# Weight sums formed again instead of reloaded, and seven chunks' state contributions formed earlier

## The chip, the cores and the metric

The kernel runs on one core of a Trainium2 chip. The metric is the device time of one execution in microseconds (us). TensorE (PE) multiplies matrices, VectorE (DVE) and ScalarE (ACT) work on tiles, GpSimd (POOL) too, and SyncE (SP) and ACT issue most transfers between the device memory and the core's own.

## The reference

One block of a network on 2048 tokens of width 1024, with 256 tokens of context ahead of it, all in 32 bits:

```python
hx = modulate(rmsnorm(x, norm1[l]), sh1, sc1)
px, qx, kx, vx, ox, gx = project(hx, w_in[l], conv_qk[l], gate_bias[l])
hc_m, st_f, st_b = mlstm_bidir(qc, kc, vc, gc, zero_state(bsz), zero_state(bsz))
hx_m, _, _ = mlstm_bidir(qx, kx, vx, gx, st_f, st_b)
pool_x = pool_mixer(px.reshape(bsz, rows, GRID_W, POOL_WIDTH), pool_w[l], pool_scale[l])
mix_x = jnp.concatenate([pool_x, mlstm_output(hx_m, ox, head_norm[l])], axis=-1) @ w_out[l]
x = x + g1 * mix_x
x = x + g2 * swiglu(modulate(rmsnorm(x, norm2[l]), sh2, sc2), w_up[l], w_down[l])
...
c_new = decay[..., None, None] * c0 + jnp.einsum('bhs,bhsv,bhsd->bhvd', wk, vc, kc)
n_new = decay[..., None] * n0 + jnp.einsum('bhs,bhsd->bhd', wk, kc)
```

The projection `w_in` has parts for the pool mixer, for queries and keys (through a convolution over three tokens), values, an output gate o, and the gates of the recurrence. The recurrence runs over the tokens forwards and backwards, in chunks; the last two lines are its state. What a chunk adds to the state (the einsum of its keys, values and weights `wk`) depends on that chunk alone; the states then follow from one another by a decay.

## The kernel before, in words

**Chunks.** The kernel takes chunks of 128 tokens: 16 of x, two of the context. For each it needs the keys transposed and weighted for both directions (`delta_a`), the products with the values of four heads (`delta_b`), copies by ACT into the state slots `ST`, and, once the neighbours are there, the decay step (`scan_step`, DVE). Slot `ST(k)` holds the forward state ahead of chunk k in partitions 0 to 63 and the backward state ahead of chunk 15 - k in the other 64.

**Units.** The pool, convolution (queries and keys) and o parts of `w_in` are computed in units of 256 columns, first for one half of the activations and then for the other. A unit multiplies two by two blocks with seven products in place of eight, and so needs seven weight operands: three are blocks of the weights, four (`SUMS`: 4, 3, 5, 2) are sums of them. Each operand is split into a high part (a cast by ACT, `wh`) and a residual (a subtraction on DVE, `wl`), and each of the seven products is 12 matmuls of 128x512 (lines 642 to 644). `operands` makes them: `wsum` forms a sum on DVE. In the first half the operands of the four sums are also stored (`keep_=s_w[w]`, line 631); in the second they are loaded again (`kept`, line 597) and only half of the second raw block is loaded. The order is: first half convolution, o, pool; second half pool, convolution, o. The activation tiles `h0` to `h6` are loaded once for a half.

**The second half's o units.** The two last units run side by side, product by product. Between the products and in their middle a hook calls `chunk_step`, which loads a later chunk's keys and values (`load_ahead`), forms `delta_a` of one chunk and `delta_b` of the one before. The state slots lie in tiles that reuse `h0`, `h1` and `h5`, so they can be written once the products with those are done. The chunks come in the order

```python
seq = [(True, cc) for cc in range(NCC)] + [(False, cc) for i in range(NCH // 2) for cc in (i, NCH - 1 - i)]
```

that is, two of the context, then 0, 15, 1, 14 and so on. What is not done by the end of the products is done behind them. Then the output weights are prepared (`load_wo`, lines 978 to 994) and the attention of the chunks begins with chunk 7 (`ml_a`, `ml_b`), whose states need all contributions; `proj` multiplies by the output weights.

**The order of instructions.** The program is given to a planner that orders each engine's instructions by the order of the program, the readiness of operands and buffers, and its own model of durations. Engines and issue queues then work in that fixed order. Buffers are given out by named pools with a number of copies; a tile waits until the earlier user of its place is done.

Of the kernel before, what the change touches and what calls it, by code (L numbers as in the profile page):

```python
# [8 lines left out]
F32 = mybir.dt.float32  # L9
# [3 lines left out]
ALU = mybir.AluOpType  # L13
# [8 lines left out]
def tile_hybrid_block(ctx: ExitStack, tc: tile.TileContext, x, c, cx, c_ctx, w_ada, b_ada, norm1, w_in, conv_qk,  # L22
                      gate_bias, pool_w, pool_scale, head_norm, w_out, norm2, w_up, w_down, norm_f, out):
    nc = tc.nc
    P = 128
# [4 lines left out]
    NCH = T // P  # L30
    NCC = TC // P
# [20 lines left out]
    dram = ctx.enter_context(tc.tile_pool(name="dram", bufs=1, space=DRAM))  # L52


    ident = const.tile([P, P], F32, name="ident")
# [68 lines left out]
    s_act = dram.tile([7, NF // 2, P, 2, 512], F32, name="s_act")  # L124
    s_t = dram.tile([7, NF // 2, P, 512], F32, name="s_t")
    s_g = dram.tile([4, D], F32, name="s_g")
    s_w = dram.tile([6, 4, 2, P, 512], F32, name="s_w")
    s_e = dram.tile([NCH // 2, P, 512], F32, name="s_e")

# [455 lines left out]
    def operands(raws, wp, early=2, keep_=None, kept=None):  # L587


        SUMS = (4, 3, 5, 2)  # L590
        if kept is not None:
            def fetch(i):
                if i in SUMS:
                    ops = [wp[0].tile([P, 4, P], F32R, name=n, bufs=5) for n in ("wh", "wl")]
                    for e, t in enumerate(ops):
                        with tc.issue_after(raw_last[0].ins):
                            nc.sync.dma_start(r32(t.rearrange("p k c -> p (k c)")), kept[SUMS.index(i), e])
                    return tuple(ops)
                src = raws[0][:, 4 * i:4 * i + 4] if i < 2 else raws[1]
                if i < early:  # L600
                    hi, lo = (vtp.tile([P, 4, P], F32R, name="vt") for _ in range(2))
                else:
                    hi = wp[0].tile([P, 4, P], F32R, name="wh", bufs=5)
                    lo = wp[0].tile([P, 4, P], F32R, name="wl", bufs=5)
                split(src, hi, lo, nc.scalar, nc.vector)
                return hi, lo
            return fetch
        A11, A12, A21, A22 = (raws[i][:, 4 * j:4 * j + 4] for i in range(2) for j in range(2))
        mem = {}

        def wsum(a, b, op):
            t = wp[0].tile([P, 4, P], F32, name="ws", bufs=3)
            nc.vector.tensor_tensor(t, a, b, op=op)  # L613
            return t

        def make(i):
            if i == 4:
                mem["s1"] = wsum(A21, A22, ALU.add)
                mem["s2"] = wsum(mem["s1"], A11, ALU.subtract)
            src = (A11 if i == 0 else A12 if i == 1 else A22 if i == 6 else mem["s2"] if i == 4 else  # L620
                   mem["s1"] if i == 3 else wsum(A11, A21, ALU.subtract) if i == 5 else
                   wsum(A12, mem["s2"], ALU.subtract))
            if i < early:
                hi, lo = (vtp.tile([P, 4, P], F32R, name="vt") for _ in range(2))
            else:
                hi = wp[0].tile([P, 4, P], F32R, name="wh", bufs=5)
                lo = wp[0].tile([P, 4, P], F32R, name="wl", bufs=5)
            split(src, hi, lo, nc.scalar, nc.vector)
            if keep_ is not None and i in SUMS:
                for e, t in enumerate((hi, lo)):  # L630
                    nc.sync.dma_start(keep_[SUMS.index(i), e], r32(t.rearrange("p k c -> p (k c)")))
            return hi, lo
        return make
# [47 lines left out]
    def load_raws(srcs, other=None, kept=False):  # L681
        raws = []
        for src in srcs:
            if other is not None and raws:
                st = other.tile([P, KD, P], F32, name="rawx")
            else:
                st = rwp.tile([P, KD, P], F32, name="raw")
            if kept and raws:
                st, src = st[:, 0:4], src[4 * P:]
            with tc.issue_after(n_last.ins):  # L690
                raw_last[0] = nc.sync.dma_start(st, src.rearrange("(k p) c -> p k c", p=P))
            raws.append(st)
        return raws

    def run_units(units, psp, wp, tmp, fetch, bg=None):


        for n, (srcs, sink, after, w, half) in enumerate(units):
            if half:
                make = operands(load_raws(srcs, kept=True), [wp], kept=s_w[w])  # L700
            else:
                make = operands(load_raws(srcs), [wp], keep_=s_w[w])
            A = {}
            for j, i in enumerate(ORDER):
                A[i] = make(i)
                if n == 0 and Btile[j] is None:
                    fetch(j)
            for j, _ in enumerate(unit(A, psp, tmp, sink)):
                if bg and (n, j) in bg:
                    bg.pop((n, j))()  # L710
            after()
# [114 lines left out]
    def o_unit(tmp, half, i0):  # L826
# [8 lines left out]
            nc.scalar.dma_start(s_so[i * P:(i + 1) * P, b * 512:(b + 1) * 512], so)  # L835
        return in_cols(O_O + i0 * P), sink, lambda: None, 4 + i0 // 2, half

    for half in range(2):
        if half:
            Btile = [None] * 7  # L840

        def fetch(j):
            if ORDER[j] < 3:
                load_B(s_hc, j, None, None)
            else:
                load_B(s_ha[half], j, wp, "hst")
        if half == 0:
            padr = ExitStack()
            adr = padr.enter_context(pool("adr2", 1))
            fins = []  # L850

            def acc(seg, n):
                return lambda: fins.append(ada_acc(seg, n, adr, 5))

            def fin():
                fins.pop()(tp, "tp")
            with pool("cvp", 1) as bp:
                run_units([conv_unit(bp, half, i0) for i0 in (2, 0)], pu_, wp, tmp, fetch, {(1, 0): acc(3, 0)})
            with pool("gp", 1) as gp:
                GI = gp.tile([P, P], F32, name="GI")  # L860
                GF = gp.tile([P, P], F32, name="GF")
                gates_to(gat, GI, GF, NCH, 64)


                mask = gat.rearrange("p c g -> p (c g)").rearrange("p (d j) -> p d j", d=2)
                nc.gpsimd.memset(mask, 0.0)
                nc.gpsimd.affine_select(out=mask[:, 0], in_=mask[:, 0], pattern=[[1, P]], compare_op=ALU.is_ge, fill=-BIG, base=0,
                                        channel_multiplier=-1)
                nc.gpsimd.affine_select(out=mask[:, 1], in_=mask[:, 1], pattern=[[-1, P]], compare_op=ALU.is_ge, fill=-BIG, base=0,
                                        channel_multiplier=1)  # L870

                gates = gate_chain(gp, gps, GI, GF, P, NCH, False)
                step = lambda: next(gates, None)
                run_units([o_unit(tmp, half, i0) for i0 in (0, 2)], pu_, wp, tmp, fetch,
                          {(0, 0): step, (0, 2): fin, (0, 3): acc(3, 1), (0, 4): step, (1, 0): step, (1, 2): fin,
                           (1, 3): acc(4, 0), (1, 4): step})
            plp = ExitStack()
            plu = pool_units(plp.enter_context(pool("plp", 1)))
            run_units(plu(0), pu_, wp, tmp, fetch, {(0, 3): fin, (0, 4): acc(4, 1), (1, 5): fin})
        else:  # L880
            run_units(plu(1), pu_, wp, tmp, fetch, {(0, 3): acc(2, 0), (1, 3): fin, (1, 4): acc(2, 1)})
            plp.close()
            rxp = pf.enter_context(pool("rx", 1, "right"))
            with pool("cvp", 1) as bp:
                run_units([conv_unit(bp, half, i0) for i0 in (2, 0)], pu_, wp, tmp, fetch, {(0, 3): fin})
            padr.close()
    tpp.close()

# [17 lines left out]
    bp = pj.enter_context(pool("pja", 1))  # L906
    tmps = (tmp, bp)

    seq = [(True, cc) for cc in range(NCC)] + [(False, cc) for i in range(NCH // 2) for cc in (i, NCH - 1 - i)]
    todo_kv, loaded = list(seq), []  # L910

    def load_ahead():
        if todo_kv:
            is_ctx, cc = todo_kv.pop(0)
            src = (s_kc, s_vc) if is_ctx else (s_k, s_v)
            kp = bp if not is_ctx and len(todo_kv) < 12 and len(todo_kv) % 4 < 2 else kvp
            loaded.append(dma_kv(kp, *src, cc, 2, kvp if is_ctx or cc in (0, NCH - 1) else None))

    for _ in range(2):
        load_ahead()  # L920
# [1 line left out]
    nc.sync.dma_start(A2, s_g[2].rearrange("(k p) -> p k", p=P))  # L922
    nc.vector.scalar_tensor_tensor(A2, A2, 1.0, vecs[:, C_N2:C_N2 + 8], op0=ALU.add, op1=ALU.mult)
    uns = [o_unit(tmps[u], 1, 2 * u) for u in range(2)]
    makes = [operands(load_raws(u[0], o, True), [wp], early=0, kept=s_w[u[3]]) for u, o in zip(uns, (None, rxp))]
    As = [{}, {}]
    steps = [unit(As[u], pu_, tmps[u], uns[u][1]) for u in range(2)]
    TA, TB = (0, 1, 2, 3, 13, 14, 15), (4, 5, 6, 9, 10, 11, 12)
# [7 lines left out]
    def ST(k):  # L936
        return sta[:, TA.index(k)] if k in TA else stb[:, TB.index(k)] if k in TB else stc[:, k - 7]
# [628 lines left out]
```

## Time and profile before

| | us |
|---|---|
| median of 3 runs | 2118.39 |
| lowest, highest | 2116.07, 2119.63 |
| the profiled execution | 2117.76 |
| its span in the trace | 2115.9 |
| PE busy in the span | 2015.6 |

The span runs from the first to the last instruction in the trace; the remaining 1.9 us of the profiled execution lie around it. All times of rows are counted from the start of the span. Idle time in a row is the time that an engine stood still just ahead of these instructions, with what ended it behind the arrow.

### The profile page before, as it was taken

Reading aid. Unit: us, or ns where it says so; the run is one execution under the profiler, and the core shown is the slowest. Engines: PE = TensorE matmul, PEld = TensorE weight load, DVE = VectorE, ACT = ScalarE, POOL = GpSimd, SP = SyncE. Lnnn points to the kernel's source line nnn. Section 1 sums busy time; section 2 is a strip of 40 time slices with the busy share of each in tenths; the row PEclk is TensorE's granted clock in tenths of the full one; section 3 lists DMA queues with packets and bytes.
Section 4 is the critical chain, followed back from the end, with each engine's and each line's share of the span. In section 5 each row is a group of like instructions: output and inputs, shape, how many; then the busy total and the mean of one; then the engine's idle time right before and its main releaser. Section 6 shows DMA issues by size and latency. Waiting matters only on the chain.

```text
span 2115.9 us, 27589 instructions
## 1 busy us (share of the span) xinstructions
PE 2015.6 (95%) x9482; PEld 1637.0 (77%) x9482; DVE 1365.8 (65%) x2333; ACT 899.1 (42%) x1787; POOL 227.0 (11%) x222
## 2 busy tenths in 40 slices
PE   7999989996999998999999999999999999999998
PEld 3997757775777776788888877888888788888887
DVE  6866868757455566666675588677677554447664
ACT  6643644456444444433333354333333343433442
POOL 1000013211333320000000000000000002004121
PEclk9999999997999999999999999999999999999999
DMA  8598989689586756433342367555565584644642
GB/s 281 169 297 270 301 269 329 219 262 254 138 253 209 241 184 183 140 124 125 100 159 85 100 217 256 189 194 189 174 199 192 190 309 149 226 139 168 226 158 100
DMA packets 365812, 421.42 MB, mean 199 GB/s; under 512 B 23924, under 2 KB 241624, under 8 KB 364904
## 3 DMA queue, kind: packets, MB, share of 16 engines
q1 hardware_dynamic: 319728, 348.22, 50.9%
q10 hardware_dynamic: 45944, 71.43, 10.5%
q8 instruction: 75, 1.23, 0.2%
q14 instruction: 65, 0.53, 0.1%
HBM read 280.45 MB, written 139.12 MB: 198 GB/s over the span
## 4 chain that ended last, share of the span: by engine, by line
PE 74%; DMA 11%; DVE 5%; ACT 4%; issue 3%; SPq 1%; POOL 1%; ACTq 0%; DVEq 0%; POOLq 0%
PE pa L642 8%; PE pa L644 8%; PE pa L643 8%; PE pdn L1392 7%; PE pdn L1393 7%; PE pdn L1394 7%; PE pg L642 4%; PE pg L643 4%; PE pg L644 4%; PE pb L642 2%; PE pb L644 2%; PE pb L643 2%; PE pm L1171 2%; PE pm L1173 2%; PE pm L1172 2%
## 5 line engine op out<-in xcount | busy, mean ns | idle before, releaser
L642 PE MATMUL pa<-h,wh 128*128 128x512 f32 x680 | 271.0, 400 | 7.6 <-ACT p L656 4.7
L644 PE MATMUL pa<-h,wl 128*128 128x512 f32 x680 | 269.8, 397 | 0.3 <-DMA wl<-s_w 0.3
L643 PE MATMUL pa<-h,wh 128*128 128x512 f32 x680 | 269.5, 397 | 0.0
L148 ACT CAST wh<-ws 128x512 fp32r<-128x512 f32 x200 | 123.5, 619 | 281.3 <-PE pg L643 154.2
L1392 PE MATMUL pdn<-ow,op 128*128 128x512 f32 x616 | 236.8, 389 | 1.0 <-ACT op L148 1.0
L1393 PE MATMUL pdn<-ow,op 128*128 128x512 f32 x616 | 237.5, 389 | 0.0
L1394 PE MATMUL pdn<-ow,op 128*128 128x512 f32 x616 | 237.5, 389 | 0.0
L151 DVE TENSOR_TENSOR op<-ra,op 128x512 fp32r<-128x512 f32 x154 | 121.6, 796 | 159.4 <-ACT op L148 159.3
L148 ACT CAST op<-ra 128x512 fp32r<-128x512 f32 x154 | 95.2, 621 | 225.9 <-PE pdn L1394 223.9
L642 PE MATMUL pg<-h,wh 128*128 128x512 f32 x448 | 177.8, 397 | 2.9 <-ACT h L148 1.7
L643 PE MATMUL pg<-h,wh 128*128 128x512 f32 x448 | 178.6, 399 | 0.9 <-DVE h L151 0.8
L644 PE MATMUL pg<-h,wl 128*128 128x512 f32 x448 | 177.5, 396 | 0.0
L151 DVE TENSOR_TENSOR wl<-ws,wh 128x512 fp32r<-128x512 f32 x200 | 136.4, 685 | 55.4 <-ACT wh L148 55.2
L642 PEld LDWEIGHTS pa<-h,wh 128*128 128x128 f32 x680 | 129.0, 190 | 43.2 <-ACT p L656 6.0
L644 PEld LDWEIGHTS pa<-h,wl 128*128 128x128 f32 x680 | 128.5, 189 | 31.1 <-issue 0.5
L643 PEld LDWEIGHTS pa<-h,wh 128*128 128x128 f32 x680 | 128.8, 189 | 30.2 <-issue 1.0
L1424 POOL TENSOR_TENSOR hr<-hr,o 128x1024 f32<-128x1024 f32 x8 | 21.7, 2734 | 1096.7 <-ACT o L1437 927.0
L1392 PEld LDWEIGHTS pdn<-ow,op 128*128 128x128 f32 x616 | 115.6, 188 | 25.5 <-ACT op L148 1.4
L1393 PEld LDWEIGHTS pdn<-ow,op 128*128 128x128 f32 x616 | 115.7, 188 | 23.9
L1394 PEld LDWEIGHTS pdn<-ow,op 128*128 128x128 f32 x616 | 115.7, 188 | 23.9
L613 DVE TENSOR_TENSOR ws<-raw 128x512 f32<-128x512 f32 x100 | 69.0, 690 | 96.3 <-DMA raw<-in_w_up_dram 92.0
L148 ACT CAST vt<-raw 128x512 fp32r<-128x512 f32 x112 | 69.2, 619 | 96.0 <-PE pb L643 41.2
(357 smaller groups left out, 4330.5 us busy)
## 6 DMA issues: line engine op xcount, KB each, us to landing
raw<-in_w_up_dram SPq DMA_DIRECT2D x88, 512.0 KB
ra<-s_act SPq DMA_DIRECT2D x66, 512.0 KB
s_act<-adaw SPq DMA_DIRECT2D x84, 256.0 KB
rwt<-s_t SPq DMA_DIRECT2D x77, 256.0 KB
adaw<-in_w_ada_dram SPq DMA_DIRECT2D x64, 256.0 KB
s_act<-g SPq DMA_DIRECT2D x63, 256.0 KB
s_hb<-hb SPq DMA_DIRECT2D x7, 1792.0 KB
hst<-s_hb ACTq DMA_DIRECT2D x48, 256.0 KB
```

What stands on the lines that cost most here:

```text
L148: nc.scalar.copy(hi, src)
L151: eng_lo.tensor_tensor(lo, src, r32(hi), op=ALU.subtract)
L613: nc.vector.tensor_tensor(t, a, b, op=op)
L642: nc.tensor.matmul(ps, lhsT=ah[:, k], rhs=B[:, 0, k], start=st, stop=False, **kw)
L643: nc.tensor.matmul(ps, lhsT=ah[:, k], rhs=B[:, 1, k], start=False, stop=False, **kw)
L644: mm_last[0] = nc.tensor.matmul(ps, lhsT=al[:, k], rhs=B[:, 0, k], start=False, stop=(k == 3), **kw)
L1171: nc.tensor.matmul(pt, lhsT=mh[:, k], rhs=w[:, 0, k % 4], start=(k == 0), stop=False)
L1172: nc.tensor.matmul(pt, lhsT=mh[:, k], rhs=w[:, 1, k % 4], start=False, stop=False)
L1173: nc.tensor.matmul(pt, lhsT=mlo[:, k], rhs=w[:, 0, k % 4], start=False, stop=(k == 7))
L1392: nc.tensor.matmul(ps, lhsT=A[:, 0, ts_], rhs=W[:, 0], start=start, stop=False)
L1393: nc.tensor.matmul(ps, lhsT=A[:, 0, ts_], rhs=W[:, 1], start=False, stop=False)
L1394: nc.tensor.matmul(ps, lhsT=A[:, 1, ts_], rhs=W[:, 0], start=False, stop=stop)
```

## The change

The sums of the o units (units 4 and 5) are no longer stored in the first half. In the second half these units load their raw blocks in full and form the sums by `wsum` and the splits, like the first half's units.

The contributions of chunks 0 to 6 are formed during the second half's two convolution units, in eight calls of `estep` between the products: keys go into quarters of the tile `rawx`, values into `hst` tiles; transposes, weighting by DVE, products, two ACT copies of 128x258 and a store of 128x516 numbers into `s_d`. The last unit's second raw block uses the same `rawx` place afterwards. In the o units the sequence is now the context, 15 down to 9, 7 and 8; with each of the chunks 15 to 9, `load_ahead` also loads the contribution of its mirror chunk from `s_d` into the two state slots, 64 partitions each.

```diff
-    s_w = dram.tile([6, 4, 2, P, 512], F32, name="s_w")
+    s_w = dram.tile([4, 4, 2, P, 512], F32, name="s_w")
+    NE = NCH // 2 - 1
+    s_d = dram.tile([NE, P, 516], F32, name="s_d")
...
-                make = operands(load_raws(srcs), [wp], keep_=s_w[w])
+                make = operands(load_raws(srcs), [wp], keep_=s_w[w] if w < 4 else None)
...
+    def early_states(room):
+        todo_e, got, begun = list(range(NE)), [], []
+        def load():
+            if todo_e:
+                cc = todo_e.pop(0)
+                kT = room[:, cc % 4]
+                nc.sync.dma_start(kT, s_k[:, cc * P:(cc + 1) * P].rearrange("(t p) c -> p t c", p=P))
+                vt = wp.tile([P, 4, 129], F32, name="hst", bufs=3)
+                nc.sync.dma_start(vt.rearrange("p h v -> p (h v)"), s_v[cc * P:(cc + 1) * P, :])
+                got.append((cc, kT, vt))
+        def estep():
+            new = None
+            if got:
+                cc, kT, vt = got.pop(0)
+                pk = gps.tile([P, 512], F32, name="gps")
+                for p_ in range(2):
+                    nc.tensor.transpose(out=pk[:, p_ * P:(p_ + 1) * P], in_=kT[:, p_, :], identity=ident)
+                kw = wp.tile([P, 4, 2, 64], F32, name="ws", bufs=3)
+                nc.vector.tensor_tensor(
...
+                new = (cc, kw, vt)
+            if begun:
+                cc, kw, vt = begun.pop(0)
+                pds = [tp.tile([P, 512], F32, name="tp") for _ in range(2)]
+                for h in range(4):
+                    hh = h % 2 * 129
+                    nc.tensor.matmul(pds[h // 2][:, hh:hh + 129], lhsT=kw[:, h].rearrange("p d c -> p (d c)"),
+                                     rhs=vt[:, h, :], start=True, stop=True)
+                dt = vtp.tile([P, 4, 129], F32, name="vt").rearrange("p h v -> p (h v)")
+                for p_ in range(2):
+                    nc.scalar.copy(dt[:, 258 * p_:258 * p_ + 258], pds[p_][:, 0:258])
+                nc.sync.dma_start(s_d[cc], dt)
+            if new:
+                begun.append(new)
+            load()
+        for _ in range(2):
+            load()
+        return estep
...
-                run_units([conv_unit(bp, half, i0) for i0 in (2, 0)], pu_, wp, tmp, fetch, {(0, 3): fin})
+                estep = early_states(rxp.tile([P, 4, 2, P], F32, name="rawx"))
+                bg = {(n, j): estep for n, js in enumerate(((0, 2, 4, 6), (0, 2, 4, 5))) for j in js}
+                bg[0, 3] = fin
+                run_units([conv_unit(bp, half, i0) for i0 in (2, 0)], pu_, wp, tmp, fetch, bg)
...
-    seq = [(True, cc) for cc in range(NCC)] + [(False, cc) for i in range(NCH // 2) for cc in (i, NCH - 1 - i)]
+    seq = [(True, cc) for cc in range(NCC)] + [(False, cc) for cc in range(NCH - 1, NCH // 2, -1)]
+    seq += [(False, NE), (False, NCH // 2)]
...
-            kp = bp if not is_ctx and len(todo_kv) < 12 and len(todo_kv) % 4 < 2 else kvp
-            loaded.append(dma_kv(kp, *src, cc, 2, kvp if is_ctx or cc in (0, NCH - 1) else None))
+            kp = bp if not is_ctx and len(todo_kv) < 5 and len(todo_kv) % 4 < 2 else kvp
+            loaded.append(dma_kv(kp, *src, cc, 2, kvp if is_ctx or cc >= NCH - 2 else None))
+            e = NCH - 1 - cc
+            if not is_ctx and e < NE:
+                nc.sync.dma_start(ST(e + 1)[0:64].rearrange("p h v -> p (h v)"), s_d[e, 0:64])
+                if e:
+                    nc.sync.dma_start(ST(NCH - e)[64:128].rearrange("p h v -> p (h v)"), s_d[e, 64:128])
...
-    makes = [operands(load_raws(u[0], o, True), [wp], early=0, kept=s_w[u[3]]) for u, o in zip(uns, (None, rxp))]
+    makes = [operands(load_raws(u[0], o), [wp], early=0) for u, o in zip(uns, (None, rxp))]
```

## Rows read from the trace of the kernel before

**Rows 1.** The page: busy us (share of the span), instructions.

```profile
PE 2015.6 (95%) x9482; PEld 1637.0 (77%) x9482; DVE 1365.8 (65%) x2333; ACT 899.1 (42%) x1787; POOL 227.0 (11%) x222
```

**Rows 2.** Stages: length, busy by engine (records), PE clock, DMA share, GB/s.

```profile
185.00:337.00 152.00, 136.05 (x544) 103.74 (x545) 117.96 (x203) 81.05 (x128) 19.28 (x46) 0.96 0.91 300
337.00:430.00 93.00, 90.64 (x381) 69.32 (x380) 72.22 (x106) 41.29 (x68) 27.39 (x25) 1.00 0.81 255
430.00:469.50 39.50, 39.33 (x196) 32.33 (x196) 20.36 (x38) 19.14 (x37) 5.78 (x4) 1.00 0.89 278
469.50:529.90 60.40, 35.60 (x171) 28.66 (x169) 44.19 (x94) 37.87 (x102) 7.89 (x5) 0.77 0.89 241
```

**Rows 3.** Timeline of the tail: start, length, engine, line, operation [idle before, releaser].

```profile
469.52 0.40 PE L644 MATMUL pa<-h,wl 128*128 128x512 f32 x1
...
513.52 0.68 DVE L151 TENSOR_TENSOR h<-big,h 128x512 fp32r<-128x512 f32 x1
...
521.08 2.55 POOL L1092 TENSOR_TENSOR raw<-raw,gat 128x1024 f32<-128x1024 f32 x1 [1.79 <-PE pqk L1090]
521.12 3.44 DVE L968 SCALAR_TENSOR_TENSOR h<-h,decx 128x129 f32<-128x129 f32 x5
...
529.88 3.53 PE L1114 MATMUL po<-vt,raw 128*128 128x129 f32 x16 [0.34 <-DVE h L1132]
```

**Rows 4.** Lines of PE, 469.5 to 529.9 us: busy, mean ns, idle before, releasers.

```profile
L958 PE MATMUL pd<-vt,kw 128*128 128x129 f32 x88 | 19.1, 373 | 13.7 <-ACT h L963 7.8 <-ACT h L148 5.2 <-DVE kw L948 0.5
L1090 PE MATMUL pqk<-h,kT 128*128 128x256 f32 x20 | 6.9, 478 | 7.5 <-DVE raw L1099 6.6 <-issue 0.8
...
L945 PE MATMUL pb<-ident,kT 128*128 128x128 f32 x10 | 2.5, 338 | 1.2 <-DVE kw L948 1.2
...
L945 PE MATMUL gps<-ident,kT 128*128 128x128 f32 x6 | 1.4, 322 | 0.0
```

**Rows 5.** The chain that ended last, 395 to 545 us: start, length, piece.

```profile
399.27 4.30 DMA s_pm<-pd
...
433.11 0.89 PE pd L958 x8
...
448.24 0.23 PE pb L945 x2
...
476.49 8.34 DMA big<-in_w_out_dram
```

**Rows 6.** DMA issues of wh, whole span: 8 for two units; wl alike.

```profile
wh<-s_w SPq DMA_DIRECT2D x24, 256.0 KB
```

**Rows 7.** Timeline where the first half's pool units begin.

```profile
304.60 1.20 POOL L773 MEMSET pu<- 128x640 f32 x2 [16.55 <-DMA s_W<-W]
...
306.01 0.79 PE L642 MATMUL pb<-h,vt 128*128 128x512 f32 x1 [6.22 <-DVE pu L794]
```

**Rows 8.** Lines of DVE and ACT over the whole span.

```profile
L151 DVE TENSOR_TENSOR wl<-ws,wh 128x512 fp32r<-128x512 f32 x200 | 136.4, 685 | 55.4 <-ACT wh L148 55.2
...
L148 ACT CAST wh<-ws 128x512 fp32r<-128x512 f32 x200 | 123.5, 619 | 281.3 <-PE pg L643 154.2 <-PE pa L643 90.3 <-DVE ws L613 16.4
...
L613 DVE TENSOR_TENSOR ws<-raw 128x512 f32<-128x512 f32 x100 | 69.0, 690 | 96.3 <-DMA raw<-in_w_up_dram 92.0 <-DMA raw<-in_w_in_dram 3.6
...
L963 ACT COPY h<-pd 64x258 f32<-64x258 f32 x60 | 22.1, 369 | 10.6 <-PE pd L958 7.4 <-DVE h L151 1.3 <-DVE kw L948 0.6
...
L968 DVE SCALAR_TENSOR_TENSOR h<-h,decx 128x129 f32<-128x129 f32 x44 | 14.9, 392 | 5.1 <-ACT h L963 5.1
...
L948 DVE TENSOR_TENSOR kw<-gps,tokq 128x512 f32<-128x512 f32 x8 | 5.5, 683 | 6.4 <-PE pd L958 6.4
```

**Rows 9.** Instructions of the tile rawx: its load, durations, first and last start.

```profile
L691 SPq DMA_DIRECT2D rawx<-in_w_in_dram x1: 383/383/383, 401.0 to 401.0; - x1
```

**Rows 10.** DMA issues between 469.5 and 529.9 us.

```profile
vt<-s_v SPq DMA_DIRECT2D x12, 258.0 KB
...
kT<-s_k SPq DMA_DIRECT2D x11, 128.0 KB
```

More of the change, by code (lines that the diff above doesn't have):

```diff
@@ L836, in o_unit @@
         return in_cols(O_O + i0 * P), sink, lambda: None, 4 + i0 // 2, half
+    def early_states(room):
[17 more added lines that the diff above has]
+                nc.vector.tensor_tensor(
+                    kw, pk[:, 0:256].rearrange("p (h d) -> p h d", h=4)[:, :, None, :].to_broadcast([P, 4, 2, 64]),
+                    tokq[:, 1, :, :, cc].rearrange("p d h -> p h d")[:, :, :, None].to_broadcast([P, 4, 2, 64]),
+                    op=ALU.mult)
+                new = (cc, kw, vt)
[16 more added lines that the diff above has]
+        return estep
     for half in range(2):
```

## The prediction, made before the changed kernel was run

> **What bounds the kernel now.** The page's busy times come first: TensorE (PE) is busy for 95% of the span and nothing else comes near [rows 1]. A change here pays only where PE waits or runs slowly, so I cut the first quarter of the kernel into stages with the window view. From 337 to 430 us PE is nearly full (90.64 of 93 us) at the full clock, and from 430 to 469.5 us too (39.33 of 39.50 us): these are the second half's pool and convolution units and the two o units. From 469.5 to 529.9 us it is busy 35.60 of 60.40 us at a mean granted clock of 0.77 [rows 2]. That stretch, from the last product of the o units to the point from which PE runs without gaps again [rows 3], I call the tail. It is where time can be won.
>
> What fills the tail shows in the lines of PE inside it. L958, the state contributions of the chunks, has 88 records; a chunk has four products and each leaves two records, so 11 of the 18 chunks still come after the o units. L945, their transposes (two groups), and L958 are busy 2.5 + 1.4 and 19.1 us, 23.0 in all (an L958 record lasts 373 ns here, part of it at the lower clock), and PE stands idle 1.2 and 13.7 us ahead of them: 37.9 of the 60.4 us belong to chunks [rows 4]. The chain of waits then says what else is in the tail: loads of the output weights, one of them 8.34 us long [rows 5], whose last operand VectorE (DVE) finishes at 514.2 us, 44 us after the o units [rows 3]. The idle time names them: 5.2 us of it ended on ACT's L148, the cast of these weights, and 7.8 us on L963, ACT's copies of the contributions, which stand in the same in-order queue as the casts [rows 4].
>
> **Part 1: the first half stores no sums for the o units.** Two units times four sums times high and low part are 16 stores of 256 KB, 4.2 MB, as large as the loads that fetch them back [rows 6], gone from a stretch whose DMA share is 0.91 [rows 2]. PE does not wait on these stores themselves; there are waits behind congested transfers. The largest is 6.22 us at 306 us, where PE waits for DVE's pool tile pu, and that for GpSimd's clearing of it, which stood behind a small store s_W from the gates [rows 7]. The stores that go are earlier than this, so the gain lies between 0 and 6.2 us. I take 2, nearer to nothing, since the pool units' stores stay.
>
> **Part 2: the o units form their sums.** 16 loads of 256 KB go. Each unit gets four sums at 690 ns (L613), four casts on ACT at 619 ns and four residuals on DVE at 685 ns [rows 8]. For two units that is 8 x 0.690 + 8 x 0.685 = 11.0 us of DVE and 5.0 us of ACT. From 430 to 469.5 us DVE is idle 39.50 - 20.36 = 19.1 us and ACT 20.4 us [rows 2]; that is the cover, and I cost the work at nothing. Without the cover, 11 us would be the loss. The second raw block of each unit is loaded in full, 0.25 MB more each. One of these blocks (rawx) takes over the buffer that the early chunks' keys now occupy; in the trace its load is issued at 401.0 us [rows 9], about 50 us before its first use. It now waits for the seventh chunk's transposes.
>
> **Part 3: seven chunks move into the convolution units.** In full-clock surroundings a chunk costs PE 0.89 us for eight L958 records and 0.23 us for two transposes [rows 5], 1.12 us together. Seven are 7.8 us, added to a stage where PE is full, so they count in full. DVE gets 7 x 0.683 = 4.8 us; ACT gets 14 copies, the nearest being L963's 369 ns, 5.2 us [rows 8]. From 337 to 430 us DVE idles 20.8 us and ACT 51.7 us [rows 2]. SP issues 14 loads and seven stores there, and 13 loads of 64 partitions in the o units; ahead of the latter in the queue nothing of PE's waits for them, but each must wait until the old activation tile is read, and what stands behind it on SP are the next chunk's keys and values.
>
> **Part 4: what is left for the tail.** Eleven chunk steps remain in the o units instead of 18. Before, seven were complete by 469.5 us; with 16 loads fewer on SP and DMA I expect nine. These two extra chunks add 2 x 1.12 = 2.2 us to the full stage. The tail then has two chunks instead of 11: nine elevenths of 23.0 us are 18.8 us of PE, and of the idle time ahead of them I take out what the weights do not cause: not the 5.2 us, only half of the 7.8 us, all of the rest, so 5.8 us times nine elevenths, 4.7 us. Together 23.5. The bounds: at most 18.8 plus nine elevenths of all 14.9 us, 31; at least what fewer transfers give (first rival), 11.
>
> **The sum**, on the profiled execution's 2117.8 us: - 2 + 7.8 + 2.2 - 23.5 = - 15.5, so 2102.3. The median of the runs shown is 0.6 us above that execution; 2103 is the forecast. Its own range is 2095 to 2111, most of the way to the bounds of the two open terms.
>
> **Rivals.** *DMA paces the tail.* In the tail the DMA engines are busy 0.89 of the time at 241 GB/s [rows 2]. 12 value and 11 key loads are issued there [rows 10]; five chunks of attention have their products in it (L1090, 20 records, four each [rows 4]) and need five of each, so at most seven value and six key loads are the chunks': 2.6 MB, 10.9 us. If the tail shortens by only that, the sum is - 2 + 10.0 - 10.9 = - 2.9, 2115. For it: the share, and that from the convolution units on as many bytes are added (0.5 MB of raw blocks, 1.85 of stored and 1.7 of reloaded contributions) as the dropped loads had, 4.2. Against it: the waits in front of PE name ACT and DVE, and only the weights' transfers lie behind them. Chance 0.18.
>
> *The other side: the early loads come late.* PE takes its work in order. If each of the seven chunks' transposes in the convolution units stands waiting for its keys for t us, the gain of 15.5 us is gone at t = 2.2 and the kernel is slower by over 0.2% from 2.8. With 4.30 us, the length of the s_pm store that PE stood behind in that stage [rows 5], it is 30 us, 2133. For it: PE has no slack there. Against it: DMA share is 0.81 in that stage and two chunks are loaded ahead. Chance 0.10.
>
> *The seven chunks do not all fit in.* If their buffer is free only near the 401 us at which rawx was loaded [rows 9], part of them, say four, slip into the o units and push as many others back into the tail. A chunk in the tail is worth 23.5 / 9 = 2.6 us, so four give back 10.4: 2113. Chance 0.10.
>
> *VectorE is held up by GpSimd.* Five scans L968 took 3.44 us while a GpSimd addition of 2.55 us ran [rows 3]; the mean of all scans of this form is 392 ns, the slow ones included [rows 8], so some 1.5 us of it or more were waiting. GpSimd is busy 5.78 us in the o units [rows 2]; if the new sums meet all of it and PE's operands are late by as much, the time is 2109. Chance 0.05. The Trainium skill, "SBUF — State Buffer", section "SBUF: two separate sides", says that a DVE operation with two SBUF inputs and a GpSimd operation that reads SBUF exclude each other for the whole instruction; by that rule all 16 added DVE operations qualify, and the trace agrees for the scans.
>
> *More than that:* the wait of 6.22 us at 306 us goes with the stores [rows 7]; 2103 less the 4.2 not yet counted is 2099. Chance 0.07.
>
> **How the numbers follow.** The forecast's case has 0.50. Less than 0.2% (4.2 us, about what a measurement of this kernel can tell) is "same". Faster: 0.50 + 0.05 + 0.07, most of the 0.10 at 2113 and a third of the first rival, 0.76. Same: the rest of these two and a little of the second rival, 0.15. Slower: 0.09, nearly all of the second rival. The range 2093 to 2116 takes in the bounds of the tail and the first and third rivals, and leaves out the second and the ends.
>
> **What would show it.** Right: between the end of the o units, some 10 us later than now, and the next stretch of full PE some 37 us pass instead of 60; L958 records after the o units fall from 88 to about 16; in the convolution units PE has some 70 new records and no new waits over 1 us; DVE's sums in the o units leave PE's idle time there under 1 us; the wait at 306 us stays. Wrong: PE idle in front of the early transposes (second rival), L958 still spread over the tail (third), a tail that is as long with few chunks in it and waits on transfers (first). An order of instructions that comes out differently elsewhere, since the program's order is planned anew, would spoil the sum by something that I can't price from these rows.

## The result and the profile after

The changed kernel takes 2130.99 us (median of four runs, 2129.73 to 2136.91); the kernel before took 2119.01 beside it (four runs, 2116.07 to 2120.59). The ratio is 1.0062, 95% interval 1.0045 to 1.0080: slower by some 12 us, where 2103 was forecast and 2116 was the end of the range. PE is still the busy engine, as in [rows 1]:

```profile
PE 2013.5 (95%) x9482; PEld 1632.4 (77%) x9482; DVE 1380.4 (65%) x2349; ACT 898.4 (42%) x1783; POOL 225.9 (11%) x222
```

The windows of the changed kernel, cut at the first product of the two convolution units and of the two o units, at the end of the o units and where PE is full again (columns as in [rows 2]):

```profile
376.80:406.30 29.50, 24.72 (x95) 17.24 (x93) 20.22 (x32) 7.25 (x12) 8.66 (x10) 1.00 0.67 211
406.30:440.80 34.50, 31.63 (x163) 25.81 (x163) 19.13 (x26) 17.56 (x31) 0.43 (x4) 0.95 0.73 215
440.80:464.80 24.00, 24.00 (x126) 19.97 (x125) 17.29 (x30) 13.18 (x25) 0.00 (x0) 1.00 0.78 223
464.80:495.70 30.90, 26.53 (x115) 20.82 (x113) 24.18 (x35) 16.15 (x31) 8.58 (x5) 0.89 0.68 196
495.70:545.60 49.90, 24.36 (x101) 18.84 (x102) 37.19 (x82) 27.66 (x77) 8.88 (x6) 0.71 0.97 244
```

The same five stretches of the kernel before:

```profile
376.20:400.00 23.80, 23.80 (x97) 17.87 (x96) 18.25 (x30) 7.81 (x13) 8.64 (x5) 1.00 0.68 215
400.00:422.70 22.70, 21.22 (x99) 17.07 (x98) 15.89 (x19) 12.40 (x17) 1.29 (x9) 1.00 0.69 211
422.70:446.30 23.60, 23.32 (x118) 19.22 (x117) 9.98 (x17) 11.53 (x22) 5.54 (x4) 1.00 0.97 317
446.30:469.90 23.60, 23.43 (x117) 18.87 (x115) 13.61 (x25) 12.70 (x27) 2.41 (x1) 1.00 0.81 236
469.90:529.90 60.00, 35.20 (x170) 28.66 (x169) 44.16 (x94) 37.87 (x102) 7.89 (x5) 0.77 0.89 240
```

Up to the convolution units the two are 0.6 us apart. The convolution units take 64.0 us instead of 46.5, the o units 54.9 instead of 47.2, and the tail to full PE 49.9 instead of 60.0. PE's idle time in that tail is as long as before (25.5 and 24.8 us); only its work is less.

Where the convolution units lose shows in the timeline, here of SP's queue, VectorE, TensorE and ScalarE in turn (start, length, what ran; in brackets the idle time before it and who ended it):

```profile
404.15 0.38 SPq L694 DMA_DIRECT2D raw<-in_w_in_dram  x1
404.62 2.07 SPq L850 DMA_DIRECT2D rawx<-s_k  x4
...
404.98 0.69 DVE L744 TENSOR_TENSOR pre<-pb,p 128x512 f32<-128x512 f32 x1 [0.86 <-DMA s_pm<-pd]
...
406.33 0.50 PE L645 MATMUL pa<-h,wh 128*128 128x512 f32 x1 [3.52 <-DVE pre L744]
...
421.00 0.62 ACT L151 CAST vt<-raw 128x512 fp32r<-128x512 f32 x1
421.52 0.38 ACT L877 COPY vt<-tp 128x258 f32<-128x258 f32 x1
424.26 0.62 ACT L151 CAST vt<-raw 128x512 fp32r<-128x512 f32 x1 [2.36 <-DMA s_d<-vt]
```

Two of these waits end on a store that frees memory. VectorE's first pre (L744) goes where the pool units' tiles lay, and it waited until the last pooled tile was stored (s_pm). And the first two operands of the second convolution unit are made in the four vt tiles (L151), in which the change also puts the early chunks' contributions (L877): the cast of 424.26 us waited 2.36 us for such a tile to be stored. The contributions are late themselves, since their keys (L850) left SP only at 404.62 us, right behind a load (L694) in front of which the queue had stood 4.8 us for VectorE. They did not need the last pooled store: in dt_inplace and late, below, they left at 399.5 and 399.0 us, before it was done. In the kernel before, products from the vt operands (pa from vt) ran up to 396.0 us and filled PE while the pool units drained; after, they run up to 428.2. The last of their lines, before and after (count, shortest, median and longest ns, first and last start):

```profile
L644 PE MATMUL pa<-h,vt x8: 389/394/802, 373.2 to 395.6; 128*128 128x512 f32 x8
L647 PE MATMUL pa<-h,vt x8: 392/396/802, 374.7 to 427.8; 128*128 128x512 f32 x8
```

So PE stood still at 402.8, until pre came. Behind this stop the granted clock was 0.50 (1.2 GHz) from 407.2 to 410.6 us.

In the second o unit VectorE is held. Two of GpSimd's mask additions (one line), two scans on VectorE, then PE:

```profile
465.96 5.27 POOL L1150 TENSOR_TENSOR raw<-raw,gat 128x1024 f32<-128x1024 f32 x2 [47.04 <-ACT h L151]
...
466.72 4.66 DVE L1026 SCALAR_TENSOR_TENSOR h<-h,decx 128x129 f32<-128x129 f32 x2
471.30 0.68 DVE L835 TENSOR_TENSOR p<-pb,p 128x512 f32<-128x512 f32 x1
...
472.03 0.69 PE L1003 MATMUL pb<-ident,kT 128*128 128x128 f32 x2 [2.95 <-DVE p L835]
```

Two scans that take 0.6 us together elsewhere end within 0.2 us of the two additions, and PE waits behind them. From 472.0 to 478.8 us PE's granted clock is 0.50.

### The profile page after: what moved, and what is told of

It reads as the page before. It is cut to its first block, busy times and chain, and to the rows that moved or that the text cites. A ratio compares the mean times of both kernels' runs of the same rounds, so it can differ in the third digit from the quotient of the medians.

```text
span 2127.0 us, 27550 instructions
## 1 busy us (share of the span) xinstructions
PE 2013.5 (95%) x9482; PEld 1632.4 (77%) x9482; DVE 1380.4 (65%) x2349; ACT 898.4 (42%) x1783; POOL 225.9 (11%) x222
## 4 chain that ended last, share of the span: by engine, by line
PE 65%; DMA 4%; DVE 2%; ACT 1%; POOL 1%; issue 1%; SPq 0%; ACTq 0%; POOLq 0%; DVEq 0%
PE pa L645 7%; PE pa L647 7%; PE pa L646 7%; PE pdn L1450 7%; PE pdn L1451 7%; PE pdn L1452 7%; PE pg L647 4%; PE pg L646 4%; PE pg L645 4%; PE pb L647 2%; PE pb L645 2%; PE pb L646 2%; DMA raw<-s_R 2%; PE pm L1229 2%; PE pm L1231 2%; PE pm L1230 2%
## 5 line engine op out<-in xcount | busy, mean ns | idle before, releaser
L151 ACT CAST wh<-ws 128x512 fp32r<-128x512 f32 x208 | 128.4, 619 | 286.5 <-PE pg L646 157.0
L151 ACT CAST op<-ra 128x512 fp32r<-128x512 f32 x154 | 95.2, 621 | 221.7 <-PE pdn L1452 219.6
L154 DVE TENSOR_TENSOR wl<-ws,wh 128x512 fp32r<-128x512 f32 x208 | 142.0, 684 | 52.7 <-ACT wh L151 50.5
L151 ACT CAST vt<-raw 128x512 fp32r<-128x512 f32 x112 | 69.0, 619 | 92.9 <-PE pb L646 41.5
```

What stands on the lines that cost most here:

```text
L151: nc.scalar.copy(hi, src)
L154: eng_lo.tensor_tensor(lo, src, r32(hi), op=ALU.subtract)
```

## The experiments

Theory A: the loss is made in the convolution units, by the tiles and the late keys above. Theory B: it is VectorE's, from the sums formed in the o units. Theory C: no single wait; PE work is added, and the tail is paced by transfers. All kernels ran beside the kernel before on the same chip; the executions of one kernel spread over 5 to 19 us, so the ratios count. "Stage" is from the first convolution product to the end of the o units, "long tail" from there to the last product of the projection (a mark that every trace has); idle is its length less PE's busy time, left are the records of chunk contributions (L958 before, L1016 after) behind the o units, eight a chunk.

| kernel | us | ratio (95%) | stage us | long tail us | idle in it | left |
|---|---|---|---|---|---|---|
| before | | 1 | 93.7 | 346.2 | 43.6 | 88 |
| after | 2130.99 | 1.0062 (1.0045-1.0080) | 118.9 | 330.1 | 43.1 | 32 |
| sums_only | 2115.68 | 0.9987 (0.9973-1.0001) | 97.3 | 341.3 | 38.1 | 88 |
| chunks_only | 2126.86 | 1.0045 (1.0027-1.0063) | 116.2 | 334.2 | 43.5 | 32 |
| dt_inplace | 2123.00 | 1.0033 (1.0015-1.0051) | 112.7 | 335.0 | 41.3 | 32 |
| late | 2117.94 | 0.9999 (0.9983-1.0015) | 113.6 | 325.1 | 38.7 | 22 |
| late_pool | 2118.32 | 0.9992 (0.9979-1.0006) | 112.2 | 326.0 | 40.5 | 22 |
| late_actq | 2123.33 | 1.0012 (1.0000-1.0025) | 111.3 | 330.3 | 44.7 | 24 |
| late_noscale | 2126.20 | 1.0039 (1.0024-1.0054) | 105.4 | 337.7 | 47.5 | 24 |
| late_halfw | 2119.75 | 0.9998 (0.9982-1.0014) | 108.7 | 332.0 | 42.9 | 22 |
| late_kt | 2113.49 | 0.9976 (0.9958-0.9995) | 109.4 | 333.8 | 45.8 | 22 |
| before_kt | 2115.16 | 0.9982 (0.9965-1.0000) | 93.8 | 338.7 | 38.4 | 88 |
| late_pool_kt | 2116.65 | 0.9992 (0.9974-1.0011) | 108.8 | 333.7 | 43.3 | 22 |
| late_stored | 2130.61 | 1.0068 (1.0047-1.0089) | 116.4 | 336.8 | 46.9 | 0 |
| late_kt_pq | 2124.90 | 1.0038 (1.0020-1.0055) | 107.5 | 335.6 | 43.7 | 22 |
| after_pool | 2132.74 | 1.0071 (1.0050-1.0091) | 116.4 | 335.2 | 46.3 | 32 |
| sums_kt | 2116.63 | 0.9993 (0.9976-1.0010) | 96.9 | 335.2 | 34.4 | 88 |
| after_nomask | 2129.37 | 1.0049 (1.0029-1.0068) | 114.2 | 335.2 | 44.1 | 32 |
| late_kt_ip | 2136.44 | 1.0075 (1.0049-1.0101) | 112.5 | 336.9 | 40.9 | 40 |

Two cautions. Stage, tail and idle time are of one execution of each kernel, which can lie off the median: late's 5.2 us below it, late_kt's 6.1 above. And each edit has the order of instructions planned anew: late_noscale, late_stored and late_kt_pq keep late's place of the chunks and are 0.4 to 0.7% slower than the kernel before. So a time alone names no cause here; it takes the wait in the trace.

**One part at a time.** sums_only is the kernel before with the sums' edits:

```
-    s_w = dram.tile([6, 4, 2, P, 512], F32, name="s_w")
+    s_w = dram.tile([4, 4, 2, P, 512], F32, name="s_w")
...
-                make = operands(load_raws(srcs), [wp], keep_=s_w[w])
+                make = operands(load_raws(srcs), [wp], keep_=s_w[w] if w < 4 else None)
...
-    makes = [operands(load_raws(u[0], o, True), [wp], early=0, kept=s_w[u[3]]) ...
+    makes = [operands(load_raws(u[0], o), [wp], early=0) ...
```

> The kernel before with the first edit alone: the o units' sums are not stored and are formed on VectorE; the chunks stay as before. Theory A (the loss sits in the convolution units, where the early chunks came): no loss here, 2115 to 2121 us, the o units still end within 3 us of where they ended before (469.9 us). Theory B (the loss is VectorE's: 11 us of new sums and the wait of 3.9 us in the o units): the o units end 5 to 8 us later and the time is 2125 to 2130. Theory C (added PE work and a tail paced by DMA, no single wait): 2115 to 2119, since fewer bytes move.

Theory A's number, and theory C's too. The o units do end later, by 6.3 us where theory A allowed 3 and theory B had 5 to 8 (51.1 us for both instead of 47.2: four scans took 3.01 us beside a mask addition of 2.35), but the long tail gives 4.9 us back. chunks_only is the mirror image, the changed kernel with these lines as before:

> The changed kernel with the sums of the o units stored and loaded again as before: only the chunks move. Theory A: the loss in the convolution units stays, so the three units' marks from 376.8 to 440.8 us are as in the changed kernel and the time is 2125 to 2131 us. Theory B: the 3.9 us of waits in the o units and more go, 2117 to 2122. Theory C: the bytes of the sums come back beside those of the chunks, 2131 to 2136.

It keeps most of the loss. Theory B falls as the main cause. Theory C's number is not met either.

**The tiles.** dt_inplace changes one line of the changed kernel:

```
-                dt = vtp.tile([P, 4, 129], F32, name="vt").rearrange("p h v -> p (h v)")
+                dt = vt.rearrange("p h v -> p (h v)")
```

> The changed kernel, but the contributions of an early chunk are copied into the tile that held the chunk's values, and not into one of the four tiles in which the second convolution unit's first operands are to be made. Theory A: the first products of that unit come early again (in front of 410 us), the two convolution units lose 8 to 10 us less, time 2121 to 2124 us. If only the late keys hold PE (theory A in part): 2128 to 2131. Theories B and C: no change, 2130 to 2132.

Stage windows of dt_inplace:

```profile
375.10:398.90 23.80, 23.80 (x96) 17.63 (x95) 19.90 (x30) 7.23 (x13) 8.47 (x6) 1.00 0.77 250
398.90:428.20 29.30, 24.76 (x116) 20.04 (x114) 17.47 (x22) 14.77 (x22) 0.80 (x8) 0.94 0.59 180
428.20:462.30 34.10, 30.69 (x154) 25.20 (x153) 18.03 (x30) 16.15 (x36) 0.99 (x2) 0.90 0.75 224
```

The first unit is full again, 23.8 us instead of 29.5, so the four tiles were what emptied it; the early chunks' work slid into the first o unit instead, which takes 34.1 us. The interval of its ratio still overlaps the changed kernel's. The wait for pre stays:

```profile
406.38 0.79 PE L645 MATMUL pb<-h,vt 128*128 128x512 f32 x1 [4.54 <-DVE pre L744]
```

**The place of the chunks.** late runs all early chunks at the second unit's yields, behind its operands in the program's order:

```
-                bg = {(n, j): estep for n, js in enumerate(((0, 2, 4, 6), (0, 2, 4, 5))) for j in js}
+                bg = {(1, j): estep for j in range(7)}
                 bg[0, 3] = fin
                 run_units([conv_unit(bp, half, i0) for i0 in (2, 0)], pu_, wp, tmp, fetch, bg)
+                estep()
```

> The changed kernel with all seven early chunks in the second convolution unit's yields and none in the first one's, so that neither their tiles nor their keys stand in front of that unit's operands. Theory A: the convolution units take 8 us more than before and not 17.5, and 2120 to 2124 us come out. Theory B: 2130 to 2132. Theory C: the same PE work in the same stretch, 2129 to 2132.

```profile
373.00:396.80 23.80, 23.80 (x95) 17.62 (x94) 19.86 (x30) 7.19 (x13) 9.34 (x6) 1.00 0.77 252
396.80:420.30 23.50, 22.92 (x112) 18.55 (x110) 17.20 (x21) 14.49 (x21) 0.80 (x8) 1.00 0.58 193
420.30:456.10 35.80, 32.99 (x178) 27.39 (x177) 21.74 (x37) 18.71 (x40) 0.99 (x2) 0.95 0.78 234
456.10:486.60 30.50, 26.58 (x127) 21.30 (x126) 26.78 (x45) 17.16 (x37) 7.64 (x3) 0.94 0.80 239
486.60:529.00 42.40, 18.85 (x85) 14.72 (x83) 33.88 (x69) 24.42 (x67) 9.91 (x5) 0.73 1.03 262
```

The loss in time is gone, more than theory A expected, and the convolution units take 47.3 us, 0.8 more than before: 40 of the 56 records of the early chunks run in the first o unit instead. The stage is 5.3 us shorter than the changed kernel's and the long tail 5.0. It is no faster than the kernel before, though: 19.9 us more of stage against 21.1 less of tail. With both waits out of the way the stage still costs twice the 10.0 us (7.8 and 2.2) of the prediction.

**What paces the tail.** late_noscale leaves out the lines that multiply the output weights on VectorE; late_halfw loads every second weight block only:

```
-                    nc.scalar.dma_start(st2, w_out[k * P:(k + 2) * P, ns].rearrange("(e p) c -> p e c", e=2))
-                st = st2[:, kk % 2]
+                    nc.scalar.dma_start(st2[:, 0], w_out[k * P:(k + 1) * P, ns])
+                src, st = st2[:, 0], st2[:, 1 - kk % 2]
...
```

> The kernel late without VectorE's multiplication of the output weights by the gate and norm vectors (16 operations of 0.72 us, 11.5 us; the output is another one). Theory V (the tail is paced by VectorE: 25.00 of 25 us busy from 500 to 525 us in late): the tail is 6 to 11 us shorter, 2106 to 2112. Theory D (by transfers): at most 2 us, 2115 to 2118.

> The kernel late with every second block of the output weights not loaded (the block before is used in its place; 2 of 4 MB, about 8 us at 240 to 270 GB/s; VectorE's and ScalarE's work is the same and the output is another one). Theory D (the tail is paced by transfers): 5 to 8 us shorter, 2109 to 2113. Theory V: at most 2 us, 2115 to 2118.

Neither V nor D: half of the weights' bytes show no effect, and without 11.5 us of VectorE work the kernel is slower: its stage is 8.2 us shorter than late's, its long tail 12.6 us longer. late_actq changes `nc.sync` to `nc.scalar` for the store of s_d:

> The kernel late, in which the early chunks' stores are issued from ScalarE's queue, right behind the copies, and not from SP's. If keys and values of the next chunks stand behind these stores on SP (in late the key loads of the o units' first chunks were issued at 434.2 and 436.0 us, behind stores, and PE waited 2.14 us for keys at 441.1), the loads come 3 to 8 us earlier, that wait goes and the time is 2113 to 2117. Rival: the loads wait for their buffers anyway, 2117 to 2119.

PE's wait for keys in the o units went, but one of 5.17 us for an operand (wl) came at 442.9 us; the time is beyond both expectations. late_stored is late with chunks_only's lines:

> The kernel late with the o units' sums stored and loaded as before. If the formed sums cost nothing beside the chunks (the sum's own assumption), the time stays within 3 us of late's 2118. If VectorE's 11 us in the o units hold PE there (theory B's remainder: 3.9 us of PE idle in late's second o unit, VectorE busy 26.78 of 30.5 us), PE's idle time there falls under 1 us and the time is 2112 to 2116, unless the bytes of the sums give it back in the tail.

A miss on both counts, and the most telling run on the tail. All 11 chunk steps ran inside the stage, none is left behind it, and yet the tail to 530 us looks like this (window, and PE's lines in it):

```profile
493.10:530.00 36.90, 16.83 (x57) 12.18 (x58) 25.42 (x58) 18.61 (x47) 6.17 (x4) 0.60 0.92 242
```

```profile
L1149 PE MATMUL pqk<-h,kT 128*128 128x256 f32 x13 | 6.0, 594 | 13.3 <-DMA h<-s_q 7.1 <-DMA kT<-s_k 6.2
L1173 PE MATMUL po<-vt,raw 128*128 128x129 f32 x16 | 3.8, 432 | 1.4 <-DVE raw L1158 1.4
```

PE is idle 20.1 of 36.9 us with no chunk in it, in front of the products of the attention and its projection. The chunks' products had filled time in which the attention's first operands were not there. late_kt (and before_kt, the kernel before with the same edit) tried to bring the first of them earlier:

```
-        kT = kp.tile([P, 2, P], F32, name="kT", bufs=bufs)
+        kT = kT0 if kp is None else kp.tile([P, 2, P], F32, name="kT", bufs=bufs)
...
+    kT0 = misc[:, 3592:3848].rearrange("p (t c) -> p t c", t=2)
...
-        kT, vt = dma_kv(m2, s_k, s_v, cc, 2)
+        kT, vt = dma_kv(m2 if n else None, s_k, s_v, cc, 2)
```

> The kernel late, in which the first attention chunk's keys have memory of their own, free during the o units, so that their load need not wait for the end of those units. In late, in late_pool and in late_noscale PE waits 6.4 to 7.4 us for these keys in front of its first attention product. Theory K (this exposed wait is what the tail kept when the chunks' products left it): the tail is 4 to 6 us shorter, 2112 to 2115 us. Theory L (the tail's first attention chunks are a chain of loads, GpSimd, ScalarE and VectorE steps that ends near 44 us behind the o units whatever its first link does): the first product comes some 6 us earlier, full PE at the same distance, 2116 to 2119.

> The kernel before with the same own memory for the first attention chunk's keys. There the products of 11 chunks stand in front of the first attention product, and these keys land before it. Theory K and theory L: no change, 2116 to 2120 us. A gain of over 4 us would say that the keys bind there too.

> late_pool and late_kt together, the candidate for a version that beats the kernel before. Theory K: 2111 to 2115 us. Theory L: 2116 to 2119.

The first attention product of late and of late_kt, and what came behind it in late_kt:

```profile
493.94 2.04 PE L1149 MATMUL pqk<-h,kT 128*128 128x256 f32 x4 [6.41 <-DMA kT<-s_k]
```

```profile
486.49 1.03 PE L1150 MATMUL pqk<-h 128*128 128x256 f32 x4
494.76 2.43 PE L1018 MATMUL pd<-vt,kw 128*128 128x129 f32 x8 [7.24 <-ACT h L1023]
```

The product came 7.4 us earlier and the next wait was as long: theory L for the mechanism. That wait stands in front of a chunk's contributions, for ScalarE's copies (L1023), ahead of which ScalarE had run weight casts and seven exponentials of the attention. The times, 0.9976 and 0.9982 of the kernel before, gain as much where no gain was expected, so they don't tell K from L; late_pool_kt (0.9992, 0.9974 to 1.0011) doesn't either. late_kt has the lowest ratio here, 5 us below the kernel before (1 to 9); sums_kt, with no chunk moved, is level with the kernel before and above its expectation:

> The kernel before with the sums formed and with own memory for the first attention chunk's keys; no chunk moves. From sums_only (ratio 0.9987) and before_kt (0.9982) together: 2110 to 2115 us where the kernel before takes 2117. If moving the chunks late is worth anything beside these, late_kt (0.9976) stays below it; if not, the two agree.

The intervals overlap: that moving the chunks late is worth anything is not shown. Last, the gate rows' loads on GpSimd's queue (`nc.gpsimd` for `nc.sync` in the load of s_R), and dt_inplace's line in late_kt:

> late_kt with the loads of the attention chunks' gate rows (s_R) issued from GpSimd's queue instead of SP's. Theory Q (full PE comes when the fourth of these loads has gone through GpSimd, ScalarE and VectorE, and its issue is late because of SP's order): it is issued near 502 us, when the first chunk's buffer is read, and full PE comes 5 to 12 us earlier, 2102 to 2109 us. Theory R (the queries and keys of the same chunk, on SP, are as late): at most 2 us, 2111 to 2114.

> late_kt with the contributions of an early chunk copied into the tile of its values, so that they take none of the four tiles that the o units' first value loads need. If these tiles still hold something up: 2108 to 2112 us where late_kt takes 2113. Rival: in the second convolution unit's yields they stand in nobody's way, 2112 to 2116.

In late_kt_pq the fourth load was issued at 498.7 us instead of 516.9, the long tail stayed (335.6 us), and the time is worse: theory Q falls, and theory R's number is missed too. In late_kt_ip an early chunk's values can be loaded only when the contributions of the chunk three before are stored, PE waits 3.42 us for pre at 404.9, five chunks are left behind the o units, and the kernel is 0.75% slower than the one before.

**GpSimd's additions.** late_pool and after_pool put an ordering hint on them:

> The kernel late, in which GpSimd's first three mask additions wait for the last copy of the chunks. If scans that run beside these additions are stretched and PE waits for it (theory B's remainder: in late one pair of scans took 2.66 us beside the addition of 463.05, another 2.06 us beside that of 472.65), no scan is longer than 0.7 us a pair in the o units, PE idles 2 to 4 us less there, and the time is 2113 to 2116 us. Rival: the additions then stand in the tail, where the first chunk of attention waits for them, and the gain is given back: 2117 to 2121.

> The changed kernel in which GpSimd's first three mask additions wait for the last copy of the chunks. If the scans stretched to 4.66 us a pair beside these additions cost the changed kernel its wait of 2.95 us at 472 us: that wait goes and the time is 2126 to 2129. Rival: the tail gives it back, 2129 to 2133.

The hint moved nothing (additions at 460.0 and 463.4, and at 464.4 and 467.2 us), so these two are repeats of late and of the changed kernel and agree with them. after_nomask leaves out the first three, and makes the exponentials behind them plain copies:

> The changed kernel without GpSimd's mask additions for the first three attention chunks, whose exponentials are plain copies (the output is another one). If the additions hold VectorE's scans (4.66 us for two at 466.72 us) and that costs the changed kernel the 2.95 us of PE's wait at 472 us: no pair of scans is longer than 0.7 us, that wait goes, 2126 to 2129 us. Rival: the time lost there is won back or lost elsewhere, 2130 to 2133.

```profile
472.71 1.13 DVE L1026 SCALAR_TENSOR_TENSOR h<-h,decx 128x129 f32<-128x129 f32 x4
...
461.20:487.40 26.20, 23.90 (x115) 18.88 (x113) 19.13 (x36) 16.19 (x31) 0.99 (x2) 1.00 0.73 230
```

No scan is stretched, and the second o unit takes 26.2 us instead of 30.9 at the full clock; but the long tail is 5.1 us longer. The time lies between the two expectations, and its interval overlaps the changed kernel's.

## Why the prediction was wrong, by its steps

**The convolution units, + 7.8: the step that failed first.** They cost 17.5 us: PE is busy 11.3 us longer there (24.72 and 31.63 us instead of 23.80 and 21.22) and idle 6.2 us longer (4.8 us in the first unit, which had none, and 2.9 instead of 1.5 in the second). What the step left out is where the chunks' tiles come from. That PE would have "no new waits over 1 us" there was argued from DMA share and from two chunks loaded ahead, and both look at transfers. The chunks themselves waited little (0.55, 0.85 and 0.32 us for VectorE in front of transposes, 0.46 for ScalarE in front of products). The product that lost its operands was another one, the second unit's first, because the contributions took vt tiles ahead of it, and so nothing covered the wait for pre, 3.52 us instead of 1.48. Of the busy time beyond 7.8 some 1.7 us is the clock (an estimate: half of the 3.4 us at 0.50); the rest, some 2 us, is not traced. dt_inplace shows the tiles by taking them away: its first unit has no idle time. late has both waits out of the way at once; no run takes away the wait for pre alone. The rival with loads that come late had the sign, and by luck the size (2133), not the mechanism; the rival of the 401 us buffer was near the time at which the keys come, but the chunks did not slip. The Trainium skill, "Perfetto Trace Analysis", section "Optimization Strategy", says that the same gap, repeating on the engine that should be full, can mean that there is no room for the next tile to be allocated; here a single gap had such a cause, with 2.36 us in front of the cast of 424.26 us.

Yet with 7.8 us here the sum as measured, below, would still be + 1.4 us and not - 15.5: the tail missed by 7.4 us and the o units by 5.5.

**The tail, - 23.5.** The long tail shortened by 16.1 us: PE's work in it by 15.7, its idle time by 0.4 (before, then after; columns as in [rows 2]):

```profile
469.90:816.10 346.20, 302.63 (x1649) 248.06 (x1648) 197.32 (x407) 161.31 (x481) 97.20 (x75) 0.94 0.71 206
495.70:825.80 330.10, 286.98 (x1580) 233.64 (x1580) 188.72 (x393) 150.72 (x455) 97.05 (x75) 0.95 0.72 210
```

Two terms failed. Nine chunks were to leave and seven did: the o units completed seven as before, so nine elevenths of 23.0 us become seven elevenths, 14.6, and 15.7 came. And the idle time ahead of the chunks' products (4.7 us of the sum) was not theirs: it was read off the lines that happened to stand in front. With no chunk left, late_stored idles PE for 46.9 us there, more than the kernel before. What paces it is not settled: not the weights' bytes, not VectorE's work on them, not the first keys, not SP's order of the s_R loads, each taken away alone. Two rivals stand untested: the loads of the attention's queries (7.1 us of late_stored's idle time ended on them) and ScalarE's queue, on which late_kt waited. A chain of the attention's first chunks through loads, GpSimd, ScalarE and VectorE fits all of these, but is argued, not shown.

**The o units, + 2.2 and sums at nothing.** No more chunks ran in them, and they cost 7.7 us: 3.9 of PE's idle time, and 3.8 of busy time at a granted clock that fell to a mean of 0.89 in the second unit. The cover was idle time of VectorE summed over the stage; it was not there at the moment of the mask addition. Yet in the end no loss shows by it: sums_only is no slower than the kernel before, and after_nomask won 4.7 us there and lost 5.1 behind. So the rival of VectorE held by GpSimd happened, with its 2.95 us of PE's wait. How much of the 12 us it explains is open: after_nomask has 1.0049 against 1.0062, with intervals that overlap, but it is still slower than the kernel before, so it is not all. The lock that the Trainium skill states ("SBUF — State Buffer", section "SBUF: two separate sides": the two operations exclude each other for the whole instruction) fits 4.66 us beside 5.27, and 0.6 us a pair in after_nomask.

**The first half's stores, - 2.** From 268.4 to 328.6 us the kernel before spent 60.2 us, the changed one 59.2 from 270.4 to 329.6. Its first part, with the stores gone, is 3.7 us shorter, and the wait behind it grew from 6.22 [rows 7] to 9.62 us: the clearing of the pool tiles that ends it, behind the small store s_W, came no sooner (306.10 us, 304.60 before). About 1 us; that wait stays, as the likeliest case had it.

The sum as measured: + 0.6 to the convolution units, + 17.5, + 7.7, - 16.1, and + 1.4 behind the long tail, 11.1 us between the two profiled executions.

## What to carry to other kernels

Before work is moved into a full stage, list the tiles that it takes there, ring by ring in program order, and ask who takes the next one and from what memory each comes free; engine and DMA shares show none of that. Work that runs in front of a wait is cover, not cost: taking it away gained its busy time here and nothing more, and idle time named in front of it stays unless what it hides is ready earlier. A stop of PE can cost more than its length, when the granted clock falls behind it. After such an edit, the cheapest test is to move the same work past the next user of its tiles.

## What the runs showed of the hardware

A VectorE scan of 128 x 129 beside a GpSimd addition of 128 x 1024 was held until the addition ended: two took 4.66 us and finished within 0.2 us of two additions of 5.27 together, and 0.6 us without one; in sums_only four took 3.01 us beside one addition of 2.35, and in after_nomask four took 1.13 without one. PE was granted the full clock in the second o unit where this was gone (1.00 instead of 0.89), at the same number of records (115); in the changed kernel its clock was 0.50 from 472.0 us on, behind an idle time of 2.95 us, and from 407.2 us on, behind one of 3.52.
